# A second Strassen product in the MLP of a two-layer encoder, taken product by product

## The chip, the cores and the metric

The kernel runs on one core of a Trainium2 chip. Its metric is the device time of one execution in microseconds (us), the median over several executions. The kernel is one program, written out in full without loops on the chip: five engines (TensorE for matrix products, VectorE, ScalarE, GpSimd, and SyncE, which issues the transfers) run their own lists of instructions in order and wait for each other on semaphores.

## The reference

The reference is a trunk of two layers over 1024 tokens of width 1024, in float32. Each layer has a token-mixing part (a short convolution, sparse attention with a top-k of keys, and banded attention), a cross-attention to 256 memory tokens, and an MLP; each ends in a layer norm of a scaled residual.

```python
def squared_relu_mlp(x, w1, w2):
    h = jnp.square(jax.nn.relu(jnp.einsum('bsd,df->bsf', x, w1)))
    return jnp.einsum('bsf,fd->bsd', h, w2)

for l in range(DEPTH):
    mix = hybrid_mixer(x, positions, w_in[l], conv_w[l], rel_bias[l], w_mix_out[l])
    x = layer_norm(ALPHA * x + mix, ln1_g[l], ln1_b[l])
    cross = memory_cross_attention(x, mem, w_mq[l], w_mkv[l], w_mo[l])
    x = layer_norm(ALPHA * x + cross, ln2_g[l], ln2_b[l])
    ff = squared_relu_mlp(x, w_ff1[l], w_ff2[l])
    x = layer_norm(ALPHA * x + ff, ln3_g[l], ln3_b[l])
```

Only the MLP, and the seams before and behind it, are touched. Its first product is 1024 x 1024 by 1024 x 4096, its second 1024 x 4096 by 4096 x 1024.

## The kernel before

**Split operands.** Every float32 factor of a large product is held as a rounded high part and a low remainder. `split` (L642 on) makes them: ScalarE casts the high part (L647), and a subtraction makes the low part (L648), on VectorE or, where the call says so, on GpSimd. `mm3` (L331 on) then issues three matmuls for one pair of operands: high by high, high by low, low by high (L333, L334, L335), 128 x 128 stationary against 512 columns.

**The first product** is already done by Strassen's algorithm (in Winograd's form). One pair of 128-feature tiles, `c` of 16, is computed for both halves of the tokens by seven products of 12 matmuls each. The operands of the tokens (`B11`, `B21`, `B22` and the sums `T1` to `T4`) are built once per layer in `x_combos`, per tile of 128 tokens, straight after the second layer norm: `then` transposes the tile on TensorE (L1522), and for tokens 512 to 1023 VectorE builds the four sums (L1540 to L1550) and the splits follow. The weights' sums `S1` to `S4` are built in `up_weights` by `make` (L1581) and split on GpSimd. `up` runs the products in the order `seq`: for the first `UP_FIRST` pairs products 1 and 2 come first, since they need no `T`; then products 6, 5, 7, 3, 4 of these pairs; then all seven of each further pair. VectorE adds each product to the partial results (L1672; product 1 is copied by ScalarE, L1670); ScalarE applies relu and square (L1634, L1635); four stores per pair send 128 x 512 blocks of `h` to DRAM (L1637).

**The second product** is a plain one. `mlp` goes through eight groups of 512 features. A group loads four 128 x 1024 rows of `h` (L1692), splits them (L1694, L1695), and for each of 8 token tiles and 2 halves of the output multiplies with four weight tiles: 12 matmuls, whose sum VectorE adds to the residual (L1737 for the first group, L1741 after it). The weight tiles come through `Weights`: a load into one of four staging buffers (L283), a cast on ScalarE (L284), a subtraction on GpSimd (L285). The last group goes tile by tile and has the layer norm (L596 to L623) and, in the first layer, the transposition for the next layer behind each tile.

**Order.** The program text gives each engine's order of priority, and a planner that estimates times may move an instruction ahead of another that is not ready. Buffers are placed by hand: `Arena` hands out addresses when the program is written out, and an instruction that writes an address waits for the last readers of what lay there before. PSUM has eight banks, given out by the one longest free. While `low` is set, as it is in the second product before and after the change, the arena takes the lowest address that has seen at least six later releases:

```python
        elif self.low and (m <= self.clock - 6).any():

            i = np.nonzero(m <= self.clock - 6)[0][0]
```

`out_proj` (L1272 on) ends the cross-attention: per tile 48 matmuls, residual and statistics on VectorE (L1300, L596), and the layer norm; the finished tiles wait in `pend` and are handed to `then`, the last four at its end.

Of the kernel before, what the change touches and what calls it, by code (L numbers as in the profile page):

```python
# [60 lines left out]
UP_FIRST = 4  # L61
# [240 lines left out]


class Kern:
    def __init__(self, ctx, tc, a):
# [11 lines left out]
        self.h = drp.tile([DFF, S], F32, name="h")  # L317
# [123 lines left out]
    def plan(self):  # L441
# [14 lines left out]
        for l in range(DEPTH):  # L456
# [45 lines left out]

            for g in range(DFF // 512):
                for d in range(2):
                    for f in range(4):
                        r = 512 * g + P * f
                        self.wi.setdefault((f"f2_{g}", l), []).append(
                            self.w.push(
                                a["w_ff2"][l, r : r + P, d * 512 : d * 512 + 512], (512,)
                            )  # L510
                        )
# [760 lines left out]
    def out_proj(self, l, key, yt, x_src, g, b, then):  # L1272
# [4 lines left out]
        for t in range(NT):  # L1277
# [28 lines left out]
            pend.append((t, x))  # L1306
        for x_ in pend:
            then(*x_)
        for x in gb:
            sb.free(x)  # L1310
# [246 lines left out]
    def up_weights(self, l):  # L1557
# [5 lines left out]
        def load(c):  # L1563
            if c in left or c >= DFF // 256:
                return
            left[c] = {"A11", "A12", "A22", "S1", "S2", "S3", "S4"}
# [30 lines left out]
        def operand(c, n):  # L1597

            if (c, n) in done:
                return  # L1600
            load(c)
            b = done[c, n] = sb.alloc(1024)
            src = quad(c, n) if n[0] == "A" else summed(c, n)
            hi, lo = (
                b.r[:, i * 512 : (i + 1) * 512].rearrange("p (k f) -> p k f", k=4)
                for i in range(2)
            )
            self.split(hi, lo, src, eng=nc.gpsimd)
            w = left[c]
# [12 lines left out]
    def up(self, l, ops, weights, late):  # L1622
# [8 lines left out]
        part, users = {}, {}  # L1631

        def out(c, f, half, b):
            nc.scalar.activation(b.ap, b.ap, AF.Relu)  # L1634
            nc.scalar.activation(b.ap, b.ap, AF.Square)  # L1635
            r = 256 * c + P * f
            nc.sync.dma_start(self.h[r : r + P, half * 512 : half * 512 + 512], b.ap)  # L1637
            sb.free(b)

        for i, (c, p) in enumerate(seq):  # L1640
            for c_, p_ in seq[i : i + 1 + UP_AHEAD]:
                operand(c_, self.PRODUCTS[p_][0])
            load(seq[min(i + 2 + 2 * UP_AHEAD, len(seq) - 1)][0])
# [3 lines left out]
            for k in range(4):  # L1647
                s = slice(k * P, (k + 1) * P)
                rh, rl = (x.r.rearrange("p (k t) -> p k t", k=4)[:, k, :] for x in ops[b])
                self.mm3(  # L1650
                    ps.ap, w.r[:, :512][:, s], w.r[:, 512:][:, s], rh, rl,
                    k == 0, k == 3,
                )
# [5 lines left out]
            for x, y, where in {  # L1659
# [3 lines left out]
                7: (("q5", "c22", (1, 1)), ("q", "q7", None)),  # L1663
# [303 lines left out]
```

## Time and profile before

| quantity | value |
|---|---|
| median of 3 runs | 3144.19 us (3140.13 to 3144.27) |
| the profiled execution, its own time | 3145.91 us |
| its span, first to last instruction | 3144.1 us |
| mean granted TensorE clock | 0.973 |
| TensorE busy | 2979.4 us (95%), 14824 matmuls |
| VectorE, ScalarE, GpSimd busy | 1913.4, 1410.7, 1367.0 us |
| bytes moved | 297.49 MB |

What lies around the span is 1.8 us of the profiled execution. A row of the profile names a line of the kernel, an engine, an operation, its output and inputs, a count, the busy time, the mean of one, and the idle time of the engine ahead of it with what ended it. Matmuls overlap in the pipeline: the time one takes from start to end is longer than the distance between two starts, and the distance is what counts.

### The profile page before, as it was taken

To read this page: it belongs to the slowest core of one execution; us is meant where nothing else is said; L and a number is where in the kernel's file an instruction comes from. 1 tells how busy PE (TensorE), PEld (TensorE's weight loads), DVE (VectorE), ACT (ScalarE), POOL (GpSimd) and SP (SyncE) were. 2 spreads that over 40 slices of the span, in tenths; PEclk is the share of its full clock that TensorE was granted. 3 is DMA by queue.
4 is the path that set the end of the run, shared out by engine and by line. 5 is a ranking of instruction groups with operands and counts; after the bars stand their busy time and mean duration, and the time that the engine had idled before them with its cause. 6 is when DMAs were issued, how large, how long until landed. Compare 5 with 4: busy or idle time off the path is not lost. (4 is left out here: it accounts for less than half of the span.)

```text
span 3144.1 us, 42269 instructions
## 1 busy us (share of the span) xinstructions
PE 2979.4 (95%) x14824; PEld 2521.0 (80%) x14824; DVE 1913.4 (61%) x3983; ACT 1410.7 (45%) x2794; POOL 1367.0 (43%) x1292
## 2 busy tenths in 40 slices
PE   8997899999979999999999978999999799999998
PEld 7886688888868888888878857887888588888886
DVE  5899888662675344333658998875526754443446
ACT  5676766433135544211356757663331455431221
POOL 4515576433255443332655174753330554432324
PEclk9998899999989999999999988999999899999999
DMA  3112132321323335222212122423222233352321
GB/s 122 54 42 58 54 113 96 131 94 60 115 81 111 111 111 207 98 103 95 88 50 69 28 59 61 125 93 124 84 92 90 74 110 112 108 209 85 114 91 64
DMA packets 201398, 297.49 MB, mean 95 GB/s; under 512 B 16865, under 2 KB 123361, under 8 KB 201185
## 3 DMA queue, kind: packets, MB, share of 16 engines
q1 hardware_dynamic: 201184, 294.78, 28.3%
q8 instruction: 117, 1.92, 0.2%
q14 instruction: 97, 0.79, 0.1%
HBM read 218.18 MB, written 70.25 MB: 92 GB/s over the span
## 5 line engine op out<-in xcount | busy, mean ns | idle before, releaser
L333 PE MATMUL banks<-sb,sb 128*128 128x512 f32 (+3 forms) x3904 | 1470.7, 379 | 25.6 <-DVE sb L648 11.7
L334 PE MATMUL banks<-sb,sb 128*128 128x512 f32 (+3 forms) x3904 | 1468.3, 377 | 4.6 <-POOL sb L285 4.6
L335 PE MATMUL banks<-sb,sb 128*128 128x512 f32 (+3 forms) x3904 | 1464.9, 377 | 0.5 <-POOL sb L648 0.5
L285 POOL TENSOR_TENSOR sb<-sb,sb 128x512 fp32r<-128x512 f32 (+2 forms) x416 | 572.8, 1392 | 963.0 <-ACT sb L284 674.8
L333 PEld LDWEIGHTS banks<-sb,sb 128*128 128x128 f32 x3904 | 740.3, 190 | 161.6 <-DVE sb L648 13.5
L334 PEld LDWEIGHTS banks<-sb,sb 128*128 128x128 f32 x3904 | 740.2, 190 | 133.0 <-POOL sb L285 6.4
L335 PEld LDWEIGHTS banks<-sb,sb 128*128 128x128 f32 x3904 | 739.0, 189 | 130.1 <-POOL sb L648 1.2
L648 POOL TENSOR_TENSOR sb<-sb,sb 128x512 fp32r<-128x512 f32 (+1 forms) x316 | 399.0, 1281 | 516.1 <-ACT sb L647 453.1
L284 ACT CAST sb<-sb 128x512 fp32r<-128x512 f32 (+2 forms) x320 | 190.3, 608 | 454.4 <-PE banks L335 283.1
L1741 DVE TENSOR_TENSOR sb<-banks,sb 128x512 f32<-128x512 f32 x224 | 153.4, 689 | 312.9 <-PE banks L335 311.8
L647 ACT CAST sb<-sb 128x512 fp32r<-128x512 f32 (+1 forms) x340 | 191.4, 588 | 287.9 <-PE banks L334 115.4
L1672 DVE TENSOR_TENSOR sb<-banks,sb 128x512 f32<-128x512 f32 x224 | 151.2, 688 | 230.4 <-PE banks L335 218.4
L647 ACT CAST sb<-banks 128x384 fp32r<-128x384 f32 (+2 forms) x324 | 160.6, 516 | 168.9 <-PE banks L1522 81.9
L648 DVE TENSOR_TENSOR sb<-banks,sb 128x384 fp32r<-128x384 f32 (+2 forms) x324 | 187.3, 594 | 69.3 <-ACT sb L647 65.1
L796 DVE TENSOR_SCALAR_CACHE_REDUCE sb<-sb,sb 128x768 bf16<-128x768 f32 (+3 forms) x256 | 207.4, 810 | 3.2 <-POOL sb L752 0.3
L997 POOL TENSOR_SCALAR sb<-sb,sb 128x128 f32<-128x128 f32 (+7 forms) x192 | 146.5, 778 | 75.5 <-DVE sb L995 70.4
L986 ACT ACTIVATE sb<-sb,sb 128x128 f32<-128x128 f32 (+7 forms) x192 | 141.8, 739 | 80.5 <-DVE sb L980 74.2
L792 ACT ACTIVATE sb<-sb,sb 128x1024 bf16<-128x1024 f32 (+1 forms) x128 | 140.4, 1097 | 47.0 <-DVE sb L815 45.6
L1694 ACT CAST sb<-sb 128x1024 fp32r<-128x1024 f32 x64 | 67.3, 1051 | 162.6 <-DMA sb<-h 84.3
L1057 PE MATMUL banks<-sb,sb 128*128 128x320 f32 (+4 forms) x288 | 83.1, 389 | 53.4 <-DVE sb L980 40.7
L1695 DVE TENSOR_TENSOR sb<-sb,sb 128x1024 fp32r<-128x1024 f32 x64 | 93.0, 1457 | 63.6 <-ACT sb L1694 62.6
L1634 ACT ACTIVATE sb<-sb 128x512 f32<-128x512 f32 x128 | 80.8, 631 | 111.7 <-DVE sb L1672 111.5
(171 smaller groups left out, 3107.8 us busy)
## 6 DMA issues: line engine op xcount, KB each, us to landing
sb<-w_ff_dram SPq DMA_DIRECT2D x128, 256.0 KB, 3.0
sb<-w_ff_dram SPq DMA_DIRECT2D x64, 512.0 KB, 3.8
h<-sb SPq DMA_DIRECT2D x128, 256.0 KB, 2.0
sb<-h SPq DMA_DIRECT2D x64, 512.0 KB, 4.1
sb<-w_in_dram SPq DMA_DIRECT2D x64, 256.0 KB, 2.9
sb<-w_mkv_dram SPq DMA_DIRECT2D x64, 256.0 KB, 2.7
xs<-sb SPq DMA_DIRECT2D x24, 512.0 KB, 2.6
sb<-xs SPq DMA_DIRECT2D x24, 512.0 KB, 3.9
```

The source lines that it names most:

```text
L284: (k.nc.vector.tensor_copy if self.late else k.nc.scalar.copy)(hi, st)
L285: k.nc.gpsimd.tensor_tensor(lo, st, hi.bitcast(F32), op=ALU.subtract)
L333: mm(out, lh, rh, start=start, stop=False)
L334: mm(out, lh, rl, start=False, stop=False)
L335: mm(out, ll, rh, start=False, stop=stop)
L647: nc.scalar.copy(hi, src)
L648: eng.tensor_tensor(lo, src, hi.bitcast(F32), op=ALU.subtract)
L796: nc.vector.tensor_scalar(junkb[:, :w], x, c, None, op0=ALU.is_ge, op1=ALU.add, accum_out=n)
L986: nc.scalar.activation(pt.ap, pt.ap, AF.Exp, bias=mn, scale=-1.0, accum_out=sm)
L997: nc.gpsimd.tensor_scalar(pt.ap, pt.ap, rc[:, i : i + 1], 0.0, op0=ALU.mult, op1=ALU.add)
L1672: nc.vector.tensor_tensor(r.ap, ps.ap, part[c, x].ap, op=ALU.add)
L1741: nc.vector.tensor_tensor(x, ps.ap, x, op=ALU.add)
```

## The change

The second product is done by Strassen's seven products too. Its quarters are: halves of the tokens against the two 128-feature tiles of every pair (for `h`), and the two tiles of a pair against halves of the 1024 outputs (for the weights). Each of the seven products runs over all 16 pairs before the next begins, for four tiles of tokens, and its sum stays in four PSUM banks; `ADDS` says to which quarters of the output it is added. The left factors of the seven products (`LEFT`) are built where `h` is made, in `up`, five sums for a pair on VectorE, and stored: seven blocks of 128 x 512 per pair instead of four. In the second product `prepare` loads, for each of the 112 steps (a product and a pair), the left block and a weight block, adds a kept weight block to it on VectorE (in five of the seven products), and splits both: the left block's low part on VectorE for even and GpSimd for odd pairs, the weights' on VectorE. It is called four steps ahead. The second product no longer uses `Weights`.

Beside that: `UP_FIRST` goes from 4 to 8, and for these pairs the two weight quarters of products 1 and 2 are loaded by themselves; the last four tiles of the second layer norm are no longer handed to `x_combos` ahead of `up` but inside it, ahead of its steps 0, 1, 2 and 4; the layer norms of the first four tiles stand within product 6, those of the last four behind a last half of product 2 that is done tile by tile; the next layer's first weights are fetched by `prefetch` between these. The diff, cut:

```diff
-UP_FIRST = 4
+UP_FIRST = 8
+DOWN_AHEAD = 4
...
-        self.h = drp.tile([DFF, S], F32, name="h")
+        self.h = drp.tile([7 * DFF // 2, 512], F32, name="h")
...
+        if hold:
+            return pend
...
+            early = c < UP_FIRST and n in ("A11", "A12")
+            if early:
+                b = sb.alloc(512)
+                src = b.ap.rearrange("p (k f) -> p k f", k=4)
+                i = 4 * (int(n[2]) - 1)
+                nc.sync.dma_start(src, v[:, i : i + 4, 256 * c : 256 * c + P])
...
+    LEFT = {
+        1: ("11", "+", "22"), 2: ("21", "+", "22"), 3: ("11",), 4: ("22",),
+        5: ("11", "+", "12"), 6: ("21", "-", "11"), 7: ("12", "-", "22"),
+    }
+    ADDS = {
+        1: ((0, 0, 1), (1, 1, 1)), 2: ((1, 0, 1), (1, 1, -1)), 3: ((0, 1, 1), (1, 1, 1)),
+        4: ((0, 0, 1), (1, 0, 1)), 5: ((0, 0, -1), (0, 1, 1)), 6: ((1, 1, 1),),
+        7: ((0, 0, 1),),
+    }
...
+        def out(c, n, b):
+            nc.scalar.activation(b.ap, b.ap, AF.Relu)
+            nc.scalar.activation(b.ap, b.ap, AF.Square)
+            if c < UP_FIRST and n == "11":
+                nc.sync.dma_start(self.h_rows(3, c), b.ap)
+                sb.free(b)
+                return
+            if c < UP_FIRST and n == "22":
+                first = quads[c, "11"] = sb.alloc(512)
+                nc.sync.dma_start(first.ap, self.h_rows(3, c))
+            quads[c, n] = b
...
+                    nc.vector.tensor_tensor(
+                        z.ap, x, y, op=ALU.add if spec[1] == "+" else ALU.subtract
+                    )
+                    nc.sync.dma_start(self.h_rows(p, c), z.ap)
...
         for i, (c, p) in enumerate(seq):
+            if pend and i in (0, 1, 2, 4):
+                combos(*pend.pop(0))
...
-        ngroup = DFF // 512
+        nk = DFF // 256
+        steps = [(p, i) for p in (5, 7, 3, 1, 4, 6, 2) for i in range(nk)]
...
+        def w2(r, d, i):
+            b = sb.alloc(512)
+            o = 256 * i + P * r
+            nc.sync.dma_start(b.ap, self.a["w_ff2"][l, o : o + P, d * 512 : d * 512 + 512])
+            return b
+
+        def prepare(n):
+            if n >= len(steps) or n in have:
+                return
+            p, i = steps[n]
+            x = sb.alloc(512)
+            nc.sync.dma_start(x.ap, self.h_rows(p, i))
+            add = nc.vector.tensor_tensor
+            if p == 5:
+                y = kept[i] = w2(1, 1, i)
+            elif p == 7:
+                y = w2(1, 0, i)
+                add(y.ap, y.ap, kept[i].ap, op=ALU.add)
...
+            res = []
+            for b, eng in ((x, nc.gpsimd if i % 2 else nc.vector), (y, nc.vector)):
+                hl = sb.alloc(1024)
+                self.split(hl.r[:, :512], hl.r[:, 512:], b.ap, eng=eng)
+                if b is x or p != 5:
+                    sb.free(b)
+                res.append(hl)
+            have[n] = res
...
+        def product(n, t, ps):
+            i = steps[n][1]
+            x, y = (b.r for b in have[n])
+            s = slice(t * P, (t + 1) * P)
+            self.mm3(
+                ps[t].ap, x[:, :512][:, s], x[:, 512:][:, s], y[:, :512], y[:, 512:],
+                i == 0, i == nk - 1,
+            )
+
+        def drop(n):
+            for b in have.pop(n):
+                sb.free(b)
...
+        half = nk // 2
+        last = len(steps) - half
+        for n, (p, i) in enumerate(steps[:last]):
+            for m in range(n, n + 1 + DOWN_AHEAD):
+                prepare(m)
+            if i == 0:
+                ps = [self.ps.alloc() for _ in range(4)]
+            for t in range(4):
+                product(n, t, ps)
+            drop(n)
+            if i == nk - 1:
+                for t in range(4):
+                    evict(p, t, ps)
+            if p == 6:
+                if i == 0:
+                    ready(0)
+                if i % 4 == 2:
+                    norm(i // 4, 2)
+        for n in range(last, len(steps)):
+            prepare(n)
+        ready(1)
...
+        for t in range(4):
+            for n in range(last, len(steps)):
+                product(n, t, ps)
+                if t == 3:
+                    drop(n)
+            evict(2, t, ps)
+            norm(4 + t, 2 if t < 1 else int(t < 3))
+            if l < DEPTH - 1:
+                self.w.prefetch(self.wi["g1", l + 1][2 * t + 1])
```

More of the change, by code (lines that the diff above doesn't have):

```diff
@@ L501, in plan @@
                     )
[L503 to L511, printed above, removed]
     def feat(self, xt, key, l):
@@ L1269, in pipeline, with out_proj @@
                 yield d * u[3]
-    def out_proj(self, l, key, yt, x_src, g, b, then):
+    def out_proj(self, l, key, yt, x_src, g, b, then, hold=False):
         nc, sb = self.nc, self.sb
@@ L1306, in out_proj @@
             pend.append((t, x))
+        for x in gb:
+            sb.free(x)
+        if hold:
+            return pend
         for x_ in pend:
             then(*x_)
-        for x in gb:
-            sb.free(x)
     def memory(self, l, st):
@@ L1677, in up @@
                 if where:
-                    out(c, *where, part.pop((c, y)))
+                    out(c, where, part.pop((c, y)))
             self.ps.free(ps)
@@ L1700, in residual @@
             xs[t] = sb.alloc(1024, top=True)
             nc.sync.dma_start(xs[t].ap, self.x2[t * P : (t + 1) * P, :])
-        def early():
-            for i in range(4):
-                fetch(0, i)
-                yield
-                self.w.get(self.wi["f2_0", l][i])
-                yield
-            while True:
-                yield
-        self.w.reserve = 0
-        self.up(l, ops, weights, early())
-        self.w.limit = None
-        self.w.reserve = 20480
-        sb.low = True
@@ new lines, in drop, with evict @@
+        def drop(n):
+            for b in have.pop(n):
+                sb.free(b)
+        def evict(p, t, ps):
+            for half, d, sign in self.ADDS[p]:
+                tt = 4 * half + t
+                x = xs[tt].ap[:, d * 512 : d * 512 + 512]
+                op = ALU.add if sign > 0 else ALU.subtract
+                if (tt, d) in begun:
+                    nc.vector.tensor_tensor(x, x, ps[t].ap, op=op)
+                else:
+                    nc.vector.scalar_tensor_tensor(
+                        x, x, ALPHA, ps[t].ap, op0=ALU.mult, op1=op
+                    )
+                    begun.add((tt, d))
+            self.ps.free(ps[t])
@@ L1759, in mlp, with norm @@
+        def norm(t, spread):
             st = self.small(12)
             for d in range(2):
-                down(g, t, d)
                 self.norm_stats(xs[t].ap, st, d)
-            if pend is not None:
-                then(*pend)
-            self.layer_norm(xs[t].ap, gb, 2 if t < NT - 3 else int(t < NT - 1), st)
-            pend = (t, xs[t])
-        for i in range(4):
-            for b in hs.pop((g, i)):
-                sb.free(b)
+            if pend:
+                then(*pend.pop())
+            self.layer_norm(xs[t].ap, gb, spread, st)
+            pend.append((t, xs[t]))
@@ L1908, in build @@
             self.w.limit = self.wi["values", l][-1] + 1
-            self.out_proj(l, "values", ot, self.xs[0], "ln2_g", "ln2_b", then)
+            pend = self.out_proj(
+                l, "values", ot, self.xs[0], "ln2_g", "ln2_b", then, hold=True
+            )
             nxt = XT(self, ())
@@ L1922, in ready @@
                     nxt.alloc(half)
-            self.mlp(l, ops, weights, ready, then)
+            self.mlp(l, ops, weights, combos, pend, ready, then)
             xt = nxt
```

140 lines of the change are left out of this document (71 added, 69 removed).

## The prediction

> **What bounds the kernel now.** I read the page first: busy times, the chain that ended last, the costliest groups.
>
> ```profile
> span 3144.1 us, 42269 instructions
> PE 2979.4 (95%) x14824; PEld 2521.0 (80%) x14824; DVE 1913.4 (61%) x3983; ACT 1410.7 (45%) x2794; POOL 1367.0 (43%) x1292
> PE 33%; DVE 2%; issue 1%; DMA 0%; ACT 0%; POOL 0%; SPq 0%; POOLq 0%; ACTq 0%; DVEq 0%
> ```
>
> TensorE (PE) is busy 95% of the span, and it carries nearly all of the chain that the view names. So a matmul removed is time removed, as long as TensorE is fed. Next, the busy time in chosen stretches: the columns after the stretch are its length and each engine's busy time with its instructions, then TensorE's granted clock, the DMA share and GB/s.
>
> ```profile
> 880.00:895.00 15.00, 12.79 (x68) 10.45 (x66) 11.45 (x17) 6.75 (x13) 6.26 (x4) 1.00 0.33 107
> 895.00:910.00 15.00, 7.08 (x24) 5.45 (x24) 15.00 (x19) 5.57 (x11) 13.34 (x9) 0.86 0.14 41
> 910.00:925.00 15.00, 7.55 (x25) 6.06 (x26) 13.71 (x19) 8.27 (x16) 7.83 (x6) 0.57 0.51 170
> 1000.00:1100.00 100.00, 100.00 (x443) 82.80 (x442) 40.42 (x58) 51.55 (x87) 47.40 (x38) 1.00 0.33 111
> 1215.00:1262.00 47.00, 47.00 (x209) 38.95 (x208) 20.76 (x25) 14.97 (x20) 10.92 (x7) 1.00 0.57 220
> 1262.00:1400.00 138.00, 138.00 (x610) 114.30 (x610) 52.99 (x64) 27.89 (x38) 40.21 (x28) 1.00 0.29 99
> ```
>
> In the first product (1000 to 1100) and in the second (1262 to 1400) TensorE never stops and the clock is full. Only where the first product begins (895 to 925) is it starved, and there its clock falls too. Now the waits, by TensorE's instructions in order of time (start, duration, idle time ahead and its end), in both layers.
>
> ```profile
> 884.27 2.78 PE L1522 MATMUL banks<-sb,sb 128*128 128x128 f32 x24
> 887.95 0.50 PE L333 MATMUL banks<-sb,sb 128*128 128x512 f32 x1 [0.90 <-ACT sb L1541]
> ...
> 899.43 0.80 PE L333 MATMUL banks<-sb,sb 128*128 128x512 f32 x1 [5.74 <-DVE sb L648]
> 900.45 0.63 PE L335 MATMUL banks<-sb,sb 128*128 128x512 f32 x1
> 900.88 0.63 PE L333 MATMUL banks<-sb,sb 128*128 128x512 f32 x1
> ...
> 916.90 1.97 PE L1522 MATMUL banks<-sb,sb 128*128 128x128 f32 x8 [10.39 <-DVE sb L623]
> ...
> 2460.52 0.80 PE L333 MATMUL banks<-sb,sb 128*128 128x512 f32 x1 [5.16 <-DVE sb L648]
> 2479.27 1.97 PE L1522 MATMUL banks<-sb,sb 128*128 128x128 f32 x8 [10.04 <-DVE sb L623]
> 2484.84 0.80 PE L333 MATMUL banks<-sb,sb 128*128 128x512 f32 x1 [3.60 <-ACT sb L647]
> 3127.05 0.39 PE L333 MATMUL banks<-sb,sb 128*128 128x512 f32 x1
> ...
> 3129.32 0.39 PE L334 MATMUL banks<-sb,sb 128*128 128x512 f32 x1
> ```
>
> The last two rows are ten starts apart: 2.27 us, so a matmul costs 0.227 us, not the 0.379 us that the groups give as its mean. (610 matmuls in 138.00 us give 0.226.) After a wait of 5 us two starts lie 0.43 us apart (900.45, 900.88).
>
> **The change part by part. Matmuls removed.** Second product before: 8 groups x 2 halves x 8 tiles x 12 = 1536 per layer. After: 7 products x 16 pairs x 4 tiles x 3 = 1344. Both layers: 384 x 0.2266 = 87.0 us less. A step of 12 matmuls is 2.72 us, a product over 16 pairs 43.5 us.
>
> **The start of the first product.** The waits quoted add up to 17.0 us in the first layer and 18.8 us in the second. Some 15 and 30 matmuls at 0.43 instead of 0.227 add 3 and 6 us, and waits under 1 us some 1 us more: 46 us in all. What is late is VectorE:
>
> ```profile
> 883.78 1.37 DVE L1300 SCALAR_TENSOR_TENSOR sb<-sb,banks 128x512 f32<-128x512 f32 x2 [3.55 <-PE banks L335]
> 915.56 1.28 DVE L623 SCALAR_TENSOR_TENSOR sb<-sb,sb,sb 128x1024 f32<-128x1024 f32 x1
> 925.96 1.18 DVE L648 TENSOR_TENSOR sb<-sb,sb 128x512 fp32r<-128x512 f32 x1
> ```
>
> From the last residual (883.78) it needs 33.1 us to the last tile's norm (916.84) and 43 us to the last `T`. After the change 16 products need no `T`: 43.5 us plus the transposes. So the `T` no longer stop TensorE. But the last tile's transposition stands ahead of step 4, which TensorE reaches after 4 x 2.72 + 2.8 (the 24 transposes at 884.27) = 13.7 us, where the norm took 33.1 with three tiles' sums between its instructions. Bounds: 0 left (the planner moves more products ahead, or the norm gets through sooner, since the sums now arrive spread out) and 19 us left per layer. I take 8, nearer the low end, as the sums no longer arrive at once. Gain: 46 - 16 = 30 us (8 to 46).
>
> **Sums and stores in the first product.** Five sums for a pair, so 160 in all; a sum like them is this one:
>
> ```profile
> L1581 DVE TENSOR_TENSOR sb<-sb,sb x96: 676/693/1807, 905.4 to 2748.1; 128x512 f32<-128x512 f32 x96
> ```
>
> 0.69 us, up to 1.81. In 100 us (5.3 pairs) they add 26 x 0.69 to 0.89 = 18 to 23 us to VectorE's 40.4: hidden under TensorE. For the first eight pairs' later products a pair lasts 5 x 2.72 = 13.6 us and asks VectorE for 6 evictions, 4 weight sums and 5 new ones (15 x 0.60 = 9.0 us) beside GpSimd's 5 x 1.29 = 6.5. That is close, so I put 2 us per layer there (0 to 14: all of it in series would be 15.5 us per pair); uncovered, the sums would cost 160 x 0.69 = 110 us. Stores go from 4 to 7 a pair on SyncE's queue, in front of the weight loads that stand behind them; the DMA share at 1000 to 1100 was 0.33, and seven stores and two loads in 19 us instead of four and two leave the queue mostly free. Nothing.
>
> **Feeding the second product** is where the change pays. Each step of 2.72 us now loads 512 KB, has two casts on ScalarE and on VectorE a sum, the weights' subtraction and every second left one. First the throughput. Rows for it: two evictions back to back (0.60 us apart), and GpSimd beside VectorE.
>
> ```profile
> 1054.64 1.29 DVE L1672 TENSOR_TENSOR sb<-banks,sb 128x512 f32<-128x512 f32 x2 [0.24 <-PE banks L335]
> 1258.86 3.52 POOL L285 TENSOR_TENSOR sb<-sb,sb 128x512 fp32r<-128x512 f32 x2
> 1260.11 4.50 POOL L285 TENSOR_TENSOR sb<-sb,sb 128x512 fp32r<-128x512 f32 x2
> 1259.45 1.78 DVE L1695 TENSOR_TENSOR sb<-sb,sb 128x1024 fp32r<-128x1024 f32 x1
> L1695 DVE TENSOR_TENSOR sb<-sb,sb x64: 1209/1226/2314, 1189.7 to 3047.8; 128x1024 fp32r<-128x1024 f32 x64
> ```
>
> The subtraction that takes 1.23 us alone took 1.78 from inside a GpSimd one, and the next GpSimd one (1260.11 to 1262.38, where 1.29 is usual) took 2.27: the two take turns. So I add them: per step VectorE 2.5 x 0.60 = 1.5, GpSimd 0.65, evictions 8 x 0.60 / 16 = 0.3, in all 2.45 of 2.72 us. It fits, at 90%.
>
> The Trainium skill, SBUF — State Buffer, "SBUF: two separate sides", says that VectorE with two SBUF inputs and GpSimd hold a shared port pair as an exclusive lock; the trace agrees (1.78 against 1.23). By full locking the step is the 2.45 us above; without any it would be VectorE's own 1.8.
>
> Second, the latency. `prepare` releases x and y, and `product`'s operands are dropped: four releases a step. An address is handed out again after six, lowest first, so the loads of step m take the addresses of step m-2, and wait until its splits are done. Two steps' time, 5.44 us, must hold one round of load, sum, cast and subtraction:
>
> ```profile
> 1258.92 0.33 SPq L283 DMA_DIRECT2D sb<-w_ff_dram  x1
> 1262.20 0.62 ACT L284 CAST sb<-sb 128x512 fp32r<-128x512 f32 x1 [0.69 <-DMA sb<-w_ff_dram]
> 1260.17 0.33 SPq L283 DMA_DIRECT2D sb<-w_ff_dram  x1
> 1263.05 0.63 ACT L284 CAST sb<-sb 128x512 fp32r<-128x512 f32 x1 [0.23 <-DMA sb<-w_ff_dram]
> sb<-w_ff_dram SPq DMA_DIRECT2D x128, 256.0 KB, 3.0
> sb<-h SPq DMA_DIRECT2D x64, 512.0 KB, 4.1
> ```
>
> From issue to use 3.28 and 2.88, mean 3.1; plus 0.69 + 0.62 + 0.69 and 0.1 between engines: 5.2 us, just inside 5.44. But every instruction meets a queue. I estimate for each of the two on VectorE 0.45 us (half an instruction ahead of it, and in a quarter of the cases the rest of a GpSimd one) and 0.2 on ScalarE: 6.3 us, 3.15 per step. Bounds: 2.72 (no queue) and, with the 4.1 us row in place of 3.1, 3.65 per step. Product 5 has no sum, and operands may run some five steps ahead (14 us); then products 7, 3, 1 and 4 lose 64 x 0.43 = 27.5, less 14: 13.5 us.
>
> Product 6 also holds four layer norms, each with two 1024-wide GpSimd instructions:
>
> ```profile
> L615 POOL TENSOR_TENSOR sb<-sb,sb x14: 2331/2401/2992, 1536.7 to 3132.4; 128x1024 f32<-128x1024 f32 x14
> ```
>
> VectorE and GpSimd in turn: 40 x 0.60 + 8 x 1.29 + 8 x 2.40 = 53.5 us against 43.5; with VectorE's own statistics, 13 us lost (0, if the operands are far enough ahead, to 25). Product 2 has no sum and catches up: 0 (to 5). Per layer 27 us, both layers 54; bounds 0 and 2 x (64 x 0.93 - 14 + 25 + 5) = 151.
>
> Gone are 128 evictions per layer for 48, and the weights' passage through staging: off the path. Behind the last matmul the same eviction and norm remain: 0.
>
> **Sum**, against the profiled execution's 3145.9 us: -87.0 - 30 + 4 + 54 = -59, so 3086.9. The median shown is 1.7 lower: 3085 us.
>
> **Rivals.** *The feed keeps up* (28%). For it: the bare round of 5.2 us and 90% of turns both fit, and TensorE never stopped in the second product before. Against it: there only 12 loads fell on 43.5 us, now some 32. The 54 us become about 5: 3036 us.
>
> *The reuse of addresses decides, and the change loses* (17%). The price is 64 steps times the excess over 2.72, product 6 included at the same rate. It decides from about 3.5 us per step (a round of 7.0): there, 64 x 0.78 - 14 = 36 plus 23 in product 6 make 59 per layer, 118 in both, and the gains of 117 are gone. At 3.6 us it is 66 per layer, 132 in both: 3145.9 - 1.7 - 87 - 30 + 4 + 132 = 3163 us. For it: the 4.1 us row for 512 KB in flight; against it: the loads, 208 x 256 KB in some 330 us, are 165 GB/s, under the 220 that 1215 to 1262 carried without a stop.
>
> *TensorE's clock falls between steps* (6%). After waits of 5 us about 14 matmuls ran at 0.43, 2.9 us each time; if 27 us per layer come as seven long waits, 7 x 2.9 x 2 = 41 us more: 3126. For it: 0.57 at 910 to 925. Against it: the matmul behind a wait of 0.90 us (887.95) lasted 0.50 us, not the 0.80 of those behind 5 us; short waits seem harmless. The Trainium skill, TensorE: Matmul & The Clock Gate, "HAM oscillation", describes this rule: waits in a loop of short bursts bring the clock to half each time; its threshold is about 3.4 us of idling, and the trace shows the half (0.43) behind 5 us.
>
> *The sums bind the first product* (3%): 14 us per layer instead of 2, 3109. That the change doesn't do what it says I leave at nothing: the counts follow from the loops.
>
> **How the numbers follow.** The forecast, 3085, has 46%, its own range 3055 to 3120. Faster by over 0.2% (6 us, about what a measurement of this kernel can tell from no change): forecast, keeping up, most of the clock and the sums: 0.79. Slower: the losing case and a tail of the clock's, 0.17; within: 0.04. The range for 8 in 10 goes from 3028 (keeping up, with half of the start's remaining wait gone) to 3150, leaving the losing case out.
>
> **What would show it.** 14440 matmuls. The stretch of product 5 in the second product full, waits behind VectorE, ScalarE or loads in products 7 to 4, the most in product 6; SyncE waiting for VectorE's subtractions ahead of the loads. Transposes L1522 of the last tile waiting under 19 us for the norm. No wait for the `T`. The forecast is wrong if TensorE is full through products 7 to 4 (rival one), or a step there takes 3.5 us or more (rival two).

## The result, and the profile after

The changed kernel takes 3178.62 us (median of four runs, 3172.12 to 3180.0), the kernel before on the same chip 3144.23. The ratio is 1.0107, 95% interval 1.0089 to 1.0124: slower by 1%, where 3085 us was forecast, and outside the range of 3028 to 3150. The profiled execution took 3179.41 us.

The page of the changed kernel, its head and its chain of waits by engine and by line:

```profile
span 3177.6 us, 43442 instructions
PE 2938.8 (92%) x14440; PEld 2459.1 (77%) x14440; DVE 2254.0 (71%) x4415; ACT 1521.1 (48%) x3050; POOL 1367.8 (43%) x1276
PE 7%; DMA 5%; DVE 4%; issue 1%; ACT 1%; POOL 0%; SPq 0%; DVEq 0%; ACTq 0%; POOLq 0%
DMA sb<-w_ff_dram 3%; PE banks L341 2%; PE banks L340 2%; PE banks L342 2%; DVE sb L645 2%; DMA sb<-h 1%; DMA h<-sb 1%; ACT sb L644 1%; POOL sb L645 0%; DVE sb L1685 0%; DVE sb L1823 0%; DVE sb L1776 0%; DMA sb<-x 0%; DVE sb L1821 0%; DVE sb L1773 0%
```

The 384 matmuls are gone. But TensorE's share of the chain fell from 33% to 7%, while loads rose from 0% to 5% (L1748 loads a weight block, L1757 a left block of `h`) and VectorE from 2% to 4%, with its subtractions (L645) and its sums of weights (L1776, L1773). These shares make up only 18% of the span, so they show where to look and no more. In the stretches below (columns as in the prediction) the first two are the start of the first product, the third its middle, the last two the seam between the two products.

```profile
895.00:910.00 15.00, 12.79 (x57) 10.32 (x57) 15.00 (x22) 8.83 (x18) 13.69 (x9) 0.95 0.37 110
910.00:925.00 15.00, 14.15 (x62) 11.31 (x62) 12.10 (x14) 9.00 (x17) 12.77 (x8) 0.94 0.51 155
1000.00:1100.00 100.00, 97.51 (x417) 78.56 (x416) 72.77 (x93) 45.08 (x79) 51.49 (x37) 0.98 0.53 176
1214.00:1222.00 8.00, 8.00 (x37) 6.64 (x36) 2.78 (x5) 1.27 (x2) 0.00 (x0) 1.00 1.02 387
1222.00:1232.00 10.00, 1.82 (x8) 1.20 (x8) 4.97 (x8) 5.23 (x9) 0.00 (x0) 0.69 1.03 392
```

Where TensorE did 7.08 and 7.55 us of work in 15 at the start of the first product, it now does 12.79 and 14.15. In the middle it issues 417 matmuls in 100 us, where it was full with 443.

The marks for a finer account are TensorE's own. Each of the seven products is 192 matmuls of lines L340 to L342, and they run in the order 5, 7, 3, 1, 4, 6, 2, so counting them shows where each product begins. The first layer, one row for each product, and product 6 of the second layer (a count takes in the matmuls that stick into a stretch at its edges and, in products 6 and 2 of the first layer, the next layer's transpositions):

```profile
1212.50:1266.40 53.90, 45.72 (x193) 37.32 (x192) 24.68 (x35) 20.54 (x35) 9.62 (x7) 0.91 0.75 263
1266.50:1310.00 43.50, 43.50 (x194) 36.03 (x193) 30.00 (x44) 16.40 (x28) 10.03 (x7) 1.00 0.50 169
1310.00:1362.10 52.10, 45.54 (x194) 35.49 (x193) 30.82 (x42) 17.30 (x30) 10.72 (x8) 1.00 0.46 153
1362.10:1416.60 54.50, 46.80 (x194) 36.42 (x192) 39.11 (x55) 20.18 (x35) 13.45 (x9) 0.97 0.45 150
1416.60:1471.20 54.60, 47.53 (x193) 36.82 (x193) 35.05 (x50) 19.27 (x34) 10.60 (x8) 0.97 0.48 163
1471.30:1542.00 70.70, 54.38 (x217) 42.01 (x216) 59.37 (x102) 28.32 (x46) 33.90 (x16) 0.86 0.44 149
1542.10:1586.70 44.60, 44.60 (x201) 36.59 (x199) 29.81 (x62) 20.04 (x37) 22.75 (x18) 1.00 0.30 91
3048.20:3116.20 68.00, 52.18 (x193) 39.79 (x192) 58.13 (x96) 25.43 (x41) 33.54 (x16) 0.87 0.44 145
```

A product is due in 43.5 us. Product 7 of the first layer keeps to that; behind it TensorE starves, most of all in product 6, where it stands still for almost a quarter of the time at a clock of 0.86 and 0.87. The same count for both layers gives this table. The column of the first product runs from the transposition of the fifth tile of tokens to the second product's first matmul.

| us, first / second layer | first product | product 5 | products 7, 3, 1, 4 | product 6 | product 2 |
|---|---|---|---|---|---|
| due | | 43.5 | 174 | 43.5 | 43.5 |
| changed kernel | 322.9 / 320.9 | 54.0 / 53.5 | 204.8 / 203.3 | 70.8 / 68.1 | 44.6 / 44.4 |

The kernel before took 330.6 and 336.5 us for the first product, and 701.1 for both second ones; the changed kernel's second ones take 743.6. So the first product gave 23.3 us, the second lost 42.5, and 14.3 more were lost ahead of the first one, between the layers and behind the last matmul: 33.5, the difference of the two spans.

Some expectations below count to VectorE's evictions instead, which come up to 15 us behind TensorE's last matmul of a product: 324.6 and 321.7 us for the first product, 334.3 and 337.9 before, 49 to 56 for each of the products 7, 3, 1 and 4.

Who waits in products 7 to 4 of the first layer (SyncE's own waits first, then those of the engines; columns: total us, times, longest):

```profile
SPq L1748 <- DVE sb L645: 90.8, 51, 5.3
SPq L1757 <- POOL sb L645: 25.8, 18, 2.7
SPq L1757 <- DVE sb L645: 12.6, 22, 2.6
```

```profile
ACT sb L644 <- DVE sb L1766: 32.1, 14, 5.6
DVE sb L1766 <- DMA sb<-w_ff_dram: 21.4, 15, 2.9
PE banks L341 <- DVE sb L645: 19.2, 14, 3.2
```

Read in a ring: a load waits on SyncE for the split that last read its address (L645), the sum (L1766) waits for the load, the cast (L644) for the sum, TensorE for the subtraction, and that subtraction is what the load two steps later waits for. VectorE is busy 134.98 of the 204.7 us, 66%. The ring does not show at once. Behind the seam TensorE waits once, for 8.18 us, and then not before 1329, when products 5 and 7 and the start of product 3 are done; VectorE had made product 7's first sum at 1246.53, 20 us before TensorE came to product 7:

```profile
1231.75 1.65 PE L340 MATMUL banks<-sb,sb 128*128 128x512 f32 x3 [8.18 <-ACT sb L644]
1329.07 0.50 PE L341 MATMUL banks<-sb,sb 128*128 128x512 f32 x1 [1.71 <-DVE sb L645]
```

### The profile page after: what moved, and what is told of

Same layout as the page of the kernel before. It is cut to its first block, busy times and chain, and to the rows that moved or that the text cites. A ratio compares the mean times of both kernels' runs of the same rounds, so it can differ in the third digit from the quotient of the medians.

```text
span 3177.6 us, 43442 instructions
## 1 busy us (share of the span) xinstructions
PE 2938.8 (92%) x14440; PEld 2459.1 (77%) x14440; DVE 2254.0 (71%) x4415; ACT 1521.1 (48%) x3050; POOL 1367.8 (43%) x1276
## 5 line engine op out<-in xcount | busy, mean ns | idle before, releaser
L341 PE MATMUL banks<-sb,sb 128*128 128x512 f32 (+3 forms) x3776 | 1438.2, 381 | 70.7 <-DVE sb L645 60.7
L340 PE MATMUL banks<-sb,sb 128*128 128x512 f32 (+3 forms) x3776 | 1432.7, 382 | 46.1 <-ACT sb L644 29.9
L342 PE MATMUL banks<-sb,sb 128*128 128x512 f32 (+3 forms) x3776 | 1423.6, 379 | 2.9 <-POOL sb L645 2.4
L645 POOL TENSOR_TENSOR sb<-sb,sb 128x512 fp32r<-128x512 f32 (+1 forms) x428 | 586.7, 1383 | 1011.4 <-ACT sb L644 896.3
L341 PEld LDWEIGHTS banks<-sb,sb 128*128 128x128 f32 x3776 | 722.9, 191 | 214.5 <-DVE sb L645 81.2
L340 PEld LDWEIGHTS banks<-sb,sb 128*128 128x128 f32 x3776 | 720.8, 191 | 185.3 <-ACT sb L644 38.3
L342 PEld LDWEIGHTS banks<-sb,sb 128*128 128x128 f32 x3776 | 721.2, 191 | 133.4 <-POOL sb L645 8.3
L644 ACT CAST sb<-sb 128x512 fp32r<-128x512 f32 (+1 forms) x788 | 454.5, 604 | 718.6 <-DMA sb<-h 142.9
L286 POOL TENSOR_TENSOR sb<-sb,sb 128x512 fp32r<-128x512 f32 (+2 forms) x288 | 382.5, 1341 | 502.8 <-ACT sb L285 408.2
L645 DVE TENSOR_TENSOR sb<-sb,sb 128x512 fp32r<-128x512 f32 x360 | 298.6, 859 | 120.9 <-ACT sb L644 114.2
L644 ACT CAST sb<-banks 128x384 fp32r<-128x384 f32 (+2 forms) x324 | 159.5, 516 | 167.0 <-PE banks L1521 80.2
L645 DVE TENSOR_TENSOR sb<-banks,sb 128x384 fp32r<-128x384 f32 (+2 forms) x324 | 187.3, 594 | 72.9 <-ACT sb L644 67.3
L1685 DVE TENSOR_TENSOR sb<-sb,sb 128x512 f32<-128x512 f32 x160 | 158.1, 1022 | 63.1 <-ACT sb L1665 61.6
L983 ACT ACTIVATE sb<-sb,sb 128x640 f32<-128x640 f32 (+7 forms) x192 | 141.6, 738 | 86.6 <-DVE sb L977 81.7
L285 ACT CAST sb<-sb 128x512 fp32r<-128x512 f32 (+2 forms) x192 | 112.0, 600 | 129.8 <-PE banks L341 29.7
L1727 DVE TENSOR_TENSOR sb<-banks,sb 128x512 f32<-128x512 f32 x224 | 149.1, 683 | 34.5 <-PE banks L342 16.5
L1582 DVE TENSOR_TENSOR sb<-sb,sb 128x512 f32<-128x512 f32 x96 | 87.0, 907 | 50.6 <-DMA h<-sb 27.8
```

Source lines behind the costliest of these rows:

```text
L286: k.nc.gpsimd.tensor_tensor(lo, st, hi.bitcast(F32), op=ALU.subtract)
L340: mm(out, lh, rh, start=start, stop=False)
L341: mm(out, lh, rl, start=False, stop=False)
L342: mm(out, ll, rh, start=False, stop=stop)
L644: nc.scalar.copy(hi, src)
L645: eng.tensor_tensor(lo, src, hi.bitcast(F32), op=ALU.subtract)
```

## The experiments

The theory (A): the round through reused addresses binds, two steps holding one round of some 6.5 us. The rival (B): the instructions of VectorE and GpSimd, which take turns, fill the step. All kernels compute the whole reference. Ratios are to the kernel before on the same chip.

**The start of the first product alone.** The kernel before with `UP_FIRST` 8, the early quarter loads and the four tiles held for `up`; its second product is left plain.

```diff
 kernel before
-UP_FIRST = 4
+UP_FIRST = 8
+            if pend and i in (0, 1, 2, 4):
+                combos(*pend.pop(0))
```

> The kernel before with only the changes at the start of the first product: eight pairs' products 1 and 2 first, their two weight quarters loaded by themselves, and the last four tiles handed on between the products. The second product is the plain one, with no new sums and four stores. In the changed kernel's trace the first product lasts 324.6 and 321.7 us between the first transposes and its last eviction, against 334.3 and 337.9 before. Theory (the waits at the start are gone whatever comes behind): 26 to 40 us faster than before, 3104 to 3120 us. Rival (the planner's other order gives part of it back elsewhere): 3125 to 3140 us.

3107.75 us, 0.9879 (0.9864 to 0.9893): 36 us faster. Its first products take 315.3 and 316.2 us, and TensorE's starved stretch is filled as in the changed kernel:

```profile
895.00:910.00 15.00, 12.77 (x59) 10.32 (x58) 15.00 (x20) 8.81 (x17) 13.94 (x9) 0.98 0.31 97
910.00:925.00 15.00, 14.15 (x61) 11.25 (x60) 12.71 (x15) 9.64 (x18) 13.14 (x8) 0.91 0.52 155
```

So the start of the first product brings 36, and all that is done for the second product turns 3107.75 into 3178.62: 71 us lost where 87 us of matmuls are saved.

**The loads' addresses alone.** Buffers under 1024 columns (the loads, the sums) are reused after 22 releases, the operands after six as in the change.

```diff
-        elif self.low and (m <= self.clock - 6).any():
+        elif self.low and (m <= self.clock - (6 if cols >= 1024 else 22)).any():
```

> The changed kernel, but in the second product the buffers of 512 columns (those that the loads fill) are handed out again only after 22 later releases instead of 6, so that the loads of a step take the addresses of a step at least six before it, not of the step two before. Nothing else is changed; the split operands of 1024 columns keep their rule. Theory A (the reuse of addresses decides): products 7, 3, 1 and 4, now 49 to 56 us each, fall to 43.5 to 45, product 6 to some 50; the second product loses 45 to 60 us less per layer; the kernel comes to 3070 to 3100 us. Theory B (VectorE and GpSimd taking turns on their time, 2.45 of 2.72 us, is what binds): the loads start earlier but nothing ends earlier, 3165 to 3180 us.

3110.55 us, 0.9882 (0.9863 to 0.99): 68 us faster than the change, with not one instruction fewer. Products 7 to 4 fall to 174.1 us in both layers: TensorE does not wait once in them, as (A) has it. The total lies 10 us above (A)'s range; product 5 (59.2 and 58.7 us) and product 6 of the first layer (65.0) still lose, while product 6 of the second layer falls to 44.4.

**All addresses at 14.** `- 14` for both sizes: the loads of a step take the addresses of the step four before it.

> The changed kernel with the distance of 6 releases set to 14 for every buffer of the second product: loads take the addresses of the step four before, and the split operands too come back later. Theory A: four steps hold a round of 10.9 us instead of 5.4, so the loads no longer bind, 3070 to 3105 us, near the run with the loads' distance alone. If the split operands' distance mattered too, this run is the faster of the two by more than 10 us. Theory B: 3165 to 3180 us.

3101.88 us, 0.9866 (0.985 to 0.9883). Products 7 to 4: 174.1 us in both layers again; product 6: 72.8 and 48.1. In products 7 to 4 of the first layer TensorE is full, and VectorE does the same work in less time, busy 76% instead of 66%:

```profile
1263.90:1437.80 173.90, 173.90 (x769) 144.00 (x768) 131.85 (x182) 68.67 (x123) 46.06 (x31) 1.00 0.55 179
```

**No GpSimd in the splits.** The left low part is always VectorE's; the distance stays six.

```diff
-            for b, eng in ((x, nc.gpsimd if i % 2 else nc.vector), (y, nc.vector)):
+            for b, eng in ((x, nc.vector), (y, nc.vector)):
```

> The changed kernel, but the left factor's low part is made on VectorE in odd pairs too, so GpSimd has no split in the second product. VectorE then has 3 x 0.60 + 0.3 = 2.1 us per step for itself and meets no GpSimd instruction outside the layer norms. Theory B (taking turns binds): the time of both together falls from 2.45 to 2.1 us per step and the kernel by 40 to 70 us, to 3110 to 3140. Theory A (reuse of addresses): the round of the weight block (load, sum, cast, subtraction) stays as it is but for the waits behind GpSimd, 3150 to 3180 us.

3131.14 us, 0.9952 (0.9935 to 0.997): 47 us faster than the change, though VectorE has half a subtraction more per step. That is in (B)'s range and 19 us under (A)'s. Yet both theories have room for it: fewer turns (B), or a round that is shorter by more than (A) had allowed. Products 7 to 4: 179.7 and 190.2 us; product 6: 69.5 and 65.0.

**Both.**

> Both edits on the changed kernel: every buffer of the second product comes back after 14 releases, and the left factor's low part is always made on VectorE. With the run that has neither (3178.6), the one with distance alone (3101.9) and the one without GpSimd alone (3131.1) this makes a table of two by two. Theory A (the round through reused addresses binds, and GpSimd only makes the round longer): with four steps for a round the GpSimd instructions no longer matter, 3090 to 3105 us, as with distance alone. Theory B (taking turns on VectorE's and GpSimd's time binds on its own): the gain of 47 us comes on top, 3050 to 3075 us.

3094.63 us, 0.9832 (0.9813 to 0.985). The four runs make a square: 3178.6, 3101.9 with the distance, 3131.1 without GpSimd, 3094.6 with both. With the distance, GpSimd is worth 7 us instead of 47: it cost the time by lengthening the round, as (A) has it. Products 7 to 4 take 174.1 us in both layers. What is left stands in product 5 (57.6 and 50.6) and in product 6 of the first layer, 70.0 us against 43.5 in the second. There TensorE stops at the next layer's transpositions (L628), each of which follows a norm. GpSimd runs the eight steps of the four norms there in one go, from 1481.72 to 1503.11, and beside it VectorE needs 2.1 us for a subtraction:

```profile
PE banks L628 <- DVE sb L636: 12.4, 1, 12.4
PE banks L628 <- POOL sb L613: 4.9, 1, 4.9
```

```profile
1485.59 19.28 DVE L645 TENSOR_TENSOR sb<-sb,sb 128x512 fp32r<-128x512 f32 x9 [3.57 <-ACT sb L644]
```

**The norms later.** The kernel with both edits, and in it the norms of the first four tiles moved from product 6 to the first half of product 2, where there is no sum.

```diff
+            if p == 2 and i % 2 == 0:
+                norm(i // 2, 2)
-                if i % 4 == 2:
-                    norm(i // 4, 2)
```

> The run with both edits, and the layer norms of the first four tiles moved from product 6 into the first half of product 2, one for two steps. Product 6 took 54 to 62 us so far where 43.5 are due. If the norms bind there, it falls to some 45 us, and product 2, which has no sums, takes up most of the norms: 10 to 20 us faster than the run with both edits. If it is only shifted, within 6 us of it.

3078.52 us, 0.9778 (0.9762 to 0.9795): 16 us less than with both edits, as expected, but not by the way that was expected. In the first layer product 6 falls from 70.0 to 43.5 us and product 2 rises from 45.2 to 67.4, with a wait of 16.0 us at L628: the loss is shifted. The 16 us come from the stretch between the layers (from the last matmul of the first layer's second product to the transposition of the fifth tile in the second layer), 868.8 us instead of 885.0.

**The order of release alone.** In the changed kernel a loop over a set releases four buffers in an order that nothing fixes; here, and in the kernels that follow, it is the order of names.

```diff
-                for m in have:
+                for m in sorted(have):
```

> The changed kernel with one difference: the tiles that a product gives back are released in the order of their names, where the order was left open, so the places of a few buffers differ. It measures how much of a difference between two kernels of this study can come from places alone. Both theories: within 10 us of the changed kernel's 3178.6, so 3169 to 3189. If it lands more than 15 us away, differences of that size between the other runs are not put down to their edits.

3176.07 us, 1.0111 (1.0096 to 1.0127). Single stages shift, though: 327.2 us for the second layer's first product instead of 320.9, 194.0 for its products 7 to 4 instead of 203.3. Differences of up to some 9 us in a stage are not read as an edit's.

**A distance of ten.** The step three before.

> The changed kernel (release in the order of names) with the distance of reuse at 10 releases for all sizes, where the change has 6 and all_far 14: the loads of a step now take the addresses of the step three before it, not two. Theory of the round: about 6.5 us (twice the 3.25 us measured per step) must fit into three steps of 2.72 us, 8.2 us, which it does with 1.7 us to spare; so nearly all that the distance of 14 brought comes already: 3095 to 3115. Rival, that every further step of distance brings its share because the feed is uneven (long GpSimd instructions, bursts of loads): about half of the gain, 3125 to 3150.

3140.11 us, 0.9983 (0.9971 to 0.9995). This missed: the total lies half way, as the rival had it, and so do products 7 to 4 with 188.3 and 181.2 us. At the distance 6 (with sorted release, 197.6 and 194.0) they lose 43 us in both layers, at 10 they lose 21, at 14 and at 22 nothing. So a round of one fixed length is too simple: three steps, 8.2 us, don't hold every round; four do.

**The norms where they were, on VectorE alone.** Distance 14, no GpSimd in the splits, and `norm(i // 4, 0)` in product 6: the two GpSimd steps of a norm go to VectorE.

> The kernel with the wide distance and without GpSimd in the splits (far_no_gpsimd, 3094.6 us), and in it the norms of the first sixteen rows' tiles in product 6 take all their work to VectorE, none to GpSimd (release in the order of names too). Theory that the two engines' turn-taking costs product 6 its time: the GpSimd steps of a norm took 2.8 us each there and made VectorE's subtractions 1.15 us long; without them VectorE's instructions go back to their alone time, and 8 to 16 us of the two layers' lost time in product 6 come back: 3079 to 3087. Theory that VectorE simply has too much to do in product 6: the norm's steps on VectorE now add 4 x about 2 us per layer to it, and the time is the same or up to 10 us worse: 3092 to 3105.

3081.48 us, 0.9809 (0.9787 to 0.9831): 13 us less than with both edits, although VectorE has more to do (the order of release differs too). Product 6 takes 47.5 us in the first layer instead of 70.0, and TensorE's waits at L628 there fall from 17.3 to 0.7 us; in the second layer it takes 47.4 instead of 43.5. Groups of instructions within product 6 of the second layer, columns busy time, then mean ns; first the changed kernel:

```profile
L612 POOL TENSOR_TENSOR sb<-sb,sb 128x1024 f32<-128x1024 f32 x4 | 11.2, 2824 | 0.0
L613 POOL TENSOR_TENSOR sb<-sb,sb 128x1024 f32<-128x1024 f32 x4 | 11.2, 2806 | 0.0
L645 DVE TENSOR_TENSOR sb<-sb,sb 128x512 fp32r<-128x512 f32 x31 | 32.5, 1085 | 6.7 <-ACT sb L644 6.6
L1776 DVE TENSOR_TENSOR sb<-sb,sb 128x512 f32<-128x512 f32 x14 | 15.9, 1142 | 3.6 <-DMA sb<-w_ff_dram 3.6
```

And with the norms on VectorE alone, where GpSimd has no instruction in the stretch:

```profile
L645 DVE TENSOR_TENSOR sb<-sb,sb 128x512 fp32r<-128x512 f32 x34 | 22.6, 681 | 0.1
L1776 DVE TENSOR_TENSOR sb<-sb,sb 128x512 f32<-128x512 f32 x8 | 5.4, 679 | 0.0
```

1.09 and 1.14 us against 0.68: beside GpSimd's 22 us, VectorE's subtractions and sums lasted some 60% longer. Here (B)'s mechanism was right, in product 6 of the first layer. With the wide distance it acts through the norm that TensorE waits for at the transpositions, not through the feed: in the second layer, which has no transpositions, product 6 was full with GpSimd's norms in it. VectorE alone feeds TensorE in products 7 to 4, and does so busy without a pause in nearly all of product 6 (1448 to 1496):

```profile
1272.20:1446.20 174.00, 174.00 (x769) 144.15 (x768) 138.73 (x224) 72.79 (x128) 0.00 (x0) 1.00 0.60 193
1448.00:1496.00 48.00, 47.31 (x220) 38.87 (x219) 48.00 (x102) 22.85 (x40) 0.00 (x0) 1.00 0.53 170
```

**Norms later and on VectorE alone**, with `norm(i // 2, 0)` in product 2:

> spread2 without the spread of the residual's loads: the norms of the first four tiles stand in product 2 and use VectorE alone, all residual loads are asked for together at the seam. Theory that the burst at the seam is what spread2 gained on: 8 to 16 us above spread2 (3053.7), 3062 to 3070, with waits at the seam of 8 us or more in at least one layer. Rival, that spread2 gained by taking GpSimd out of the moved norms: within 6 us of spread2, 3048 to 3060, the seam's waits small here too.

3064.44 us, 0.9744 (0.9728 to 0.976): 14 us less than the norms later with GpSimd (here too with the other order of release): product 2 of the first layer takes 47.3 us instead of 67.4. Its longest waits at the seam are 12.1 and 6.9 us, as the theory of the burst has it.

**The residual's loads spread, norms later.** At the seam the change asks for eight residual loads of 512 KB at once. Here each is asked for behind the load of a step, from step 4 on, the norm's constants behind step 36. (On the kernel with both edits alone, whose norms stay in product 6, the spread was to be measured too; that kernel needs more SBUF than there is and gave no time.)

```diff
         for t in range(NT):
             xs[t] = sb.alloc(1024, top=True)
-            nc.sync.dma_start(xs[t].ap, self.x2[t * P : (t + 1) * P, :])
-        gb = self.ln_consts("ln3_g", "ln3_b", l)
+        gb = []
...
+            if n < NT:
+                with self.tc.issue_after(mark[0].ins):
+                    nc.sync.dma_start(xs[n].ap, self.x2[n * P : (n + 1) * P, :])
+            if n == 32:
+                with self.tc.issue_after(mark[0].ins):
+                    gb += self.ln_consts("ln3_g", "ln3_b", l)
```

> norms_later (3078.5 us) with two edits: the norms that were moved into product 2 use VectorE alone, and the loads of the residual (8 of 512 KB per layer) are no longer asked for together at the seam between the two products but one at a time behind the loads of steps 4 to 12; the constants of the norm behind step 36. Theory that the burst at the seam delays the first small loads: the seam's waits on TensorE (10.3 and 5.3 us in layer 1 of norms_later, 8.2 and 6.5 in the changed kernel) go to under 3 us per layer, worth 8 to 16 us: 3062 to 3071. Rival, that the seam waits because the feed itself starts too late there (its first loads, sums and splits are a chain of their own): the waits stay, and the time is within 6 us of 3078.5.

3053.73 us, 0.9719 (0.9705 to 0.9734): the fastest of all, 2.8% under the kernel before. It beat the expectation because it differs from norms_later in two edits; against the kernel just above, which has the other one, the spread is worth 11 us, of which product 5 of the first layer gives 13.4 while that of the second takes 5.4 back. TensorE waited 8.18 us at the seam of the first layer in the changed kernel; its waits there now (1190 to 1262):

```profile
PE banks L340 <- ACT sb L644: 1.0, 1, 1.0
```

Product 5 takes 44.9 us there, instead of 54.0, and every product behind it is full. In the second layer the spread did not help: 57.8 us, with this wait (2715 to 2780), whose cause was not looked for:

```profile
PE banks L340 <- ACT sb L644: 12.0, 2, 10.0
```

**The same spread, norms in product 6** (VectorE alone):

> norms_vec (this call) with the residual's loads spread in the same way. Theory of the burst: 8 to 16 us below norms_vec. Rival: within 6 us of norms_vec. Set beside spread2 it also tells whether the place of the norms (product 6 or product 2) still matters when GpSimd takes no part in them: if the turn-taking was the whole cost, spread3 and spread2 are within 6 us of each other; if VectorE's load in product 6 is a cost too, spread2 is 8 us or more faster.

3079.93 us, 0.9804 (0.9789 to 0.9819): no gain over the 3081.48 without the spread, so the theory of the burst missed here. Product 5 of the first layer did shrink, from 56.5 to 47.3 us, but product 6 there grew from 47.5 to 58.9, with 8.7 us of waits at the transpositions, and the stretch between the layers from 879.1 to 885.6. In that stretch stands TensorE's longest wait from 1180 to 1600, behind product 2, for a norm of the last tiles:

```profile
PE banks L628 <- DVE sb L613: 12.7, 1, 12.7
```

That norm's last step (L613) stood on VectorE behind the last tile's L617, one of 42 such instructions. Their median is 1.28 us; this one took 8.30, beside GpSimd instructions that followed each other without a pause (rows of VectorE, then of GpSimd):

```profile
1542.45 8.30 DVE L617 SCALAR_TENSOR_TENSOR sb<-sb,sb,sb 128x1024 f32<-128x1024 f32 x1
1550.74 1.21 DVE L613 TENSOR_TENSOR sb<-sb,sb 128x1024 f32<-128x1024 f32 x1
```

```profile
1542.45 2.48 POOL L286 TENSOR_TENSOR sb<-sb,sb 128x512 fp32r<-128x512 f32 x2
1544.89 2.34 POOL L612 TENSOR_TENSOR sb<-sb,sb 128x1024 f32<-128x1024 f32 x1
1547.18 2.48 POOL L286 TENSOR_TENSOR sb<-sb,sb 128x512 fp32r<-128x512 f32 x2
```

The stretch between the layers is 869 to 874 us in the three kernels with the norms in product 2 and 877 to 892 in all others with the change's second product. So spread2's 26 us over this kernel lie in product 6 of the first layer (15) and between the layers (16), less some 5 elsewhere. In spread2 TensorE's waits at the transpositions between the layers make 7.0 us instead of 12.7; where the rest of the 16 comes from stays open.

## Why the prediction was wrong

**Matmuls removed, -87:** right, 14440 matmuls, and where TensorE is fed 192 of them take 43.5 us, 0.227 each.

**Start of the first product, -30, and its sums, +4:** together -26, and the first products became 23.3 us shorter. That the two agree is partly luck. Apart, both were too small: the start alone brought 36, and with sums and stores the first products take 7.6 and 4.7 us more than without, 12 in place of 4. There is no wait for `T` and none for the last tile's norm. Where 5.74 and 10.39 us of waiting stood, two short waits are left:

```profile
908.32 0.71 PE L340 MATMUL banks<-sb,sb 128*128 128x512 f32 x1 [2.21 <-DVE sb L645]
908.83 0.63 PE L341 MATMUL banks<-sb,sb 128*128 128x512 f32 x1
909.25 0.63 PE L342 MATMUL banks<-sb,sb 128*128 128x512 f32 x1
...
913.78 0.49 PE L340 MATMUL banks<-sb,sb 128*128 128x512 f32 x1 [0.85 <-DVE sb L645]
914.12 0.39 PE L341 MATMUL banks<-sb,sb 128*128 128x512 f32 x1
914.35 0.40 PE L342 MATMUL banks<-sb,sb 128*128 128x512 f32 x1
```

VectorE's subtraction that ends just before 908.32 reads a PSUM bank, and is thus that of a late tile's `B22`, which the products 1 and 2 that run here do not use. So it seems to be the bank that TensorE waits for; no run tests that.

**Feeding the second product, +54:** this step failed. The second products are 42.5 us longer in place of 33 shorter, so feeding cost 130. From the table, against what is due:

| us, both layers | forecast | measured |
|---|---|---|
| products 7, 3, 1, 4 | 27 | 60 |
| product 6 | 26 | 52 |
| seam and product 5 | 0 | 21 |
| product 2 | 0 | 2 |

(204.8 + 203.3 - 348 = 60; 70.8 + 68.1 - 87 = 52; 54.0 + 53.5 - 87 = 21; 44.6 + 44.4 - 87 = 2. Some 4 us of these 135 are the next layer's transpositions, which stood in the second product before too.)

In products 7 to 4 the round was named rightly, and the runs with a wider distance show it: without it they lose nothing. Two sizes were off. With the lead mostly used up, in products 3, 1 and 4, a step took 3.36 us in the first layer and 3.27 in the second (161.2 / 48 and 156.8 / 48), where 3.15 was forecast. And the lead was credited with 14 us per layer. It was there: product 7 loses nothing in the first layer and 3.1 us in the second. But it paid for 10 and 6 us (64 x 0.64 - 30.7 and 64 x 0.55 - 29.2), not 14.

Product 6 was priced by busy time, VectorE and GpSimd in turn. What counted was the round, which goes on there and which the norms make longer: 68.1 us in the second layer, 4.3 a step. With the loads' addresses farther apart and the same instructions it is 44.4 us, so the engines' time fits. The instructions were mis-sized as well, at 2.40 us for GpSimd's and at alone-times for VectorE's; beside each other they took 2.8 and 1.1. The Trainium skill, SBUF — State Buffer, "SBUF: two separate sides", calls this an exclusive lock, and the stretch without GpSimd agrees with that. In the first layer the wait at the next layer's transpositions had no term at all; it shows once the distance is wide.

The seam had none either. The sentence "Product 5 has no sum" overlooked what is asked for at its start. From 1214 to 1232 the DMA engines are full, at 387 and 392 GB/s. The issues of the changed kernel from 1205 to 1232 (count, size, us from issue to landing; the eight of 512 KB are the residual's):

```profile
sb<-x SPq DMA_DIRECT2D x8, 512.0 KB, 6.9
sb<-w_ff_dram SPq DMA_DIRECT2D x6, 256.0 KB, 6.2
sb<-h SPq DMA_DIRECT2D x5, 256.0 KB, 5.1
```

A block of `h` or of the weights takes 5.1 and 6.2 us there where the page gives 2.9 and 3.1 over the whole kernel, and TensorE waited 8.2 us. That these loads made the wait, the spread shows for the first layer; for the second it doesn't.

**The rivals.** *The reuse of addresses decides* (17%) is the mechanism that happened, and 3163 was nearer than 3085; but its point of decision, 3.5 us per step, was not reached in products 7 to 4: the step was 3.36 and 3.27, and the loss came with the seam and product 6. (Its 23 us for product 6 are not "the same rate", which gives 16 x 0.78 = 12.) *The clock falls between steps* (6%) was priced at 41 us and had a part: in the second products 48 and 67 matmuls start 0.40 to 0.46 us behind the one before, 23 us more than at full clock. How much of it TensorE would have waited anyway, the runs don't show. *The feed keeps up* (28%) failed for the kernel as it stood; with distance, VectorE alone and the spread it happens, and 3054 us is near the 3036 it priced.

**The remaining 14 us** (5 ahead of the first MLP, 5 between the layers, 4 behind the last matmul) were costed at nothing. The stretch between the layers varies from 869 to 892 us over these kernels.

## What to carry to other kernels

When buffers are handed out by reuse distance, compare the distance in steps with the whole round of load, sum, cast and subtraction, and give it the slack of its longest rounds: here 6 to 14 releases were worth 77 us, without one instruction less. A lead is spent once; behind it the stage runs at the pace of the round. Look at what else is asked for where a stage begins. Mark the stages by the engine that carries the time: counted to VectorE's evictions, products 7 to 4 would still seem to lose 14 and 13 us at the distance of 14, where TensorE loses nothing. Where two engines take turns at the same memory, a step moved to the busier engine can be a gain, as long as that engine alone still fits.

## What the runs showed of the hardware

A wait of 2.21 us was enough for half the clock: the matmuls behind 908.32 start 0.43 us apart, those behind the wait of 0.85 us (913.78) 0.23 after the first. The prediction had seen this only behind 5 us. The Trainium skill, TensorE: Matmul & The Clock Gate, "HAM oscillation", gives about 3.4 us of idling; here less sufficed, and the measurement decides. Nor does the length of the wait decide alone: in the changed kernel's second products six starts at 0.43 us follow a wait of 1.49 us, and none follows one of 1.91 us (at 1356.85).

```profile
2973.68 0.80 PE L341 MATMUL banks<-sb,sb 128*128 128x512 f32 x1 [1.49 <-DVE sb L645]
2974.28 0.63 PE L342 MATMUL banks<-sb,sb 128*128 128x512 f32 x1
2974.70 0.63 PE L340 MATMUL banks<-sb,sb 128*128 128x512 f32 x1
```

VectorE can run without a pause (48.00 of 48.00 us) while TensorE beside it loses 0.7: 66% busy, in the changed kernel, was starvation, and 100% was not. And beside GpSimd one VectorE instruction can lose far more than one turn: 8.30 us where 1.28 is the median, with five GpSimd instructions beside it.
